# A decoder trunk's FFN: four segments of 11 blocks with three fours per layer by seven products, turns in pairs, and zero matmuls in the last norm

## The chip, the cores and the metric

The kernel runs on one core of one Trainium2 chip. The time of a run is the device time in microseconds (us). PE is the tensor engine's matmuls, PEld its weight loads, DVE the vector engine, ACT the scalar engine, POOL GpSimd, and SP the engine whose queue issues the loads.

## The reference, cut to what matters

Two layers work on 256 positions of 2048 features: one with latent attention, one with dilated window attention. Each is followed by a feed-forward network with a short convolution, and after both layers comes a norm.

```python
def conv_ffn(h, w_up, conv_w, conv_b, w_down):
    u = h @ w_up                                  # 256 x 2048 by 2048 x 11264
    up = jnp.pad(u, ((0, 0), (2, 0), (0, 0)))
    c = conv_b + up[:, 0:S] * conv_w[0]
    for j in range(1, 3):
        c = c + up[:, j:j + S] * conv_w[j]
    gate, val = c[..., :5632], c[..., 5632:]
    return (jax.nn.silu(gate) * val) @ w_down     # 256 x 5632 by 5632 x 2048
...
for i in range(2):
    x = x + mixer(rms_norm(x, attn_norm[i]))
    x = x + conv_ffn(rms_norm(x, ffn_norm[i]), ...)
return rms_norm(x, final_norm)
```

The precision of float32 is kept by splitting each operand into a rounded part and a rest (high and low part) and adding three products.

## The kernel before, in words

The hidden width of 5632 is 44 blocks of 128 features. A block has a gate half and a value half. `up(fb)` makes both, one *unit* each: `load` brings 2048 columns of weights into a tile `w` (three buffers), ACT rounds them into tiles `wh` of 1024 columns (L91), DVE subtracts to get the rests `wl` (L92), with five buffers of each, and `proj` runs 16 matmuls of 512 columns over the high parts and 16 of 256 columns over the low parts, all at L135. `keep` then takes the sum out of PSUM (L211, L213), scales it, and `conv` applies the convolution: one ACT instruction (L949) and two on DVE (L953) per half, then silu on the gate half (L955), the product with the value half (L958), and `split_act` for high and low part (L346, L347). The result `gl[fb]` is one input of the down projection.

The down projection runs in segments of blocks (`SEGS`). `down(seg)` makes 16 chunks of 128 output features, one unit each, over the blocks of the segment. Each chunk's PSUM is seeded with half of the residual (L124), and `keep_residual` (L365, L367) writes the sum back into it. A segment is done after two blocks of the next one. In the last segment the first two chunks run over all inputs but the last before anything else, so that the last block has time to be finished.

Some groups of four blocks are not made by `up` but by `seven(fb0)`: the product of 2x2 blocks by Strassen's scheme in Winograd's form, 7 products instead of 8. Its stationary operands are sums of input chunks, made once per layer by `make_forms` (DVE L816 to L819, L347), for eight pairs of chunks, one in every fourth unit from the third one on. Six of the products run inside the segment that is computed at that time: after each of the 16 down units one function of `mains` is called, in turn `first(kk)` (12 matmuls, L845 to L847) and `second(kk)` (6 matmuls). `first` loads 1 MB for the pair in two halves (L865), subtracts on DVE (L873), and makes high and low parts (ACT L872, L874, DVE L875, L876); `second` makes one more difference and its parts (L884 to L887). `sums` adds the products up, `third` runs the seventh product in two halves, and `turn(f)` turns a block from positions by features to features by positions: four transposes into the one PSUM bank `pt` (L938) and the convolutions of both halves out of it.

The order of the work around this is given by the list `steps`: `unit` runs a projection, then calls the next step, then evacuates the projection before. Instructions are put into each engine's queue by a planner that follows the order of the program as far as operands and buffers are free in its own reckoning; each engine then works its queue in that order.

At the end `rstd_x` sums the squares by four matmuls, takes the root on POOL, `spread` copies the two columns over all partitions by four matmuls (L290), and DVE scales the 16 chunks, which are then stored (L1037, L1038). The kernel begins with nine matmuls on zeros (L232).

Of the kernel before, what the change touches and what calls it, by code (L numbers as in the profile page):

```python
# [18 lines left out]
F32 = mybir.dt.float32  # L19
F32R = mybir.dt.float32r  # L20
BF16 = mybir.dt.bfloat16
# [5 lines left out]
P = 128  # L27
T = 256
# [9 lines left out]
GROUPS = ((128, 1), (512, 4), (2048, 16))  # L38
FFN = 5632
FB = FFN // P  # L40
SEGS = ((0, 14), (14, 28), (28, 44))
HALF = 4 * P
SEVEN = (16, 30)
NEG = -1.0e30


# [6 lines left out]
def trunk_kernel(tc, x_d, pos_d, gain_d, conv_d, const_d, mask_d, wqa_d, wkva_d, wqb_d, wkvb_d, wo_d,  # L53
                 win_d, dwo_d, wup_d, wdn_d, out_d):
    nc = tc.nc
    with ExitStack() as ctx:
# [6 lines left out]
        work = ctx.enter_context(tc.tile_pool(name="work", bufs=4))  # L63
        small = ctx.enter_context(tc.tile_pool(name="small", bufs=4))
        pp = ctx.enter_context(tc.tile_pool(name="pp", bufs=4, space=PSUM))
        pss = ctx.enter_context(tc.tile_pool(name="pss", bufs=2, space=PSUM))
# [121 lines left out]
        steps = []  # L188
# [4 lines left out]
        def together(*fs):  # L193
            return lambda: [f() for f in fs]

        def flush():
            while pending:
                e, ps = pending.pop(0)
                e(ps)
# [27 lines left out]
        zero = work.tile([P, T], F32, name="zero", tag="lo", bufs=2)  # L227
        nc.vector.memset(zero, 0.0)
        zero = zero.bitcast(BF16)
        idle = pss.tile([P, 512], F32, name="idle", tag="ps")  # L230
        for _ in range(9):
            nc.tensor.matmul(idle, zero[:, :P], zero, start=True, stop=True)  # L232

        load_x(0, 1, nc.scalar)
        nc.scalar.dma_start(gains, gain_d)
# [40 lines left out]
        def sumsq(name, paired=False, last=None):  # L276
            acc = state[name]
            acc = acc.rearrange("p (a e) -> p e a", e=2) if paired else acc.rearrange("p (e a) -> p e a", e=2)
            ps = pso.tile([P, 512], F32, name="po", tag="po")
            for tt in range(2):  # L280
                nc.tensor.matmul(ps[:, tt:tt + 1], acc[:, tt, :], ones, start=True, stop=last is None)
                if last is not None:
                    nc.tensor.matmul(ps[:, tt:tt + 1], last[:, ts(tt, P)], ones, start=False, stop=True)
            return ps[:, 0:2]

        def spread(col, name, pool):

            ps = pso.tile([P, 512], F32, name="po", tag="po")
            for tt in range(2):
                nc.tensor.matmul(ps[:, ts(tt, P)], col[:, tt:tt + 1].to_broadcast([P, P]), ident,  # L290
                                 start=True, stop=True)
            if pool is None:
                return ps[:, :T]
            t = pool.tile([P, T], F32, name=name, tag=name)
            nc.vector.tensor_copy(t, ps[:, :T])
            return t

        def rstd_x(paired=False, last=None):
            ps = sumsq("x", paired, last)
            ms = small.tile([P, 2], F32, name="ms", tag="ms")  # L300
            nc.vector.tensor_scalar(ms, ps, 1.0 / D, EPS, op0=ALU.mult, op1=ALU.add)
            r = small.tile([P, 2], F32, name="rcol", tag="rcol")
            nc.gpsimd.tensor_tensor(r, ms, negh, op=ALU.pow)
            return r
# [57 lines left out]
        def keep_residual(k, ps, paired=False):  # L362

            t = work.tile([P, T], F32, name="lo", tag="lo", bufs=2)
            nc.scalar.activation(t, ps[:, T:], AF.Copy)  # L365
            hi, lo = (a.rearrange("p (e a) -> p e a", e=2) for a in (ps[:, :T], t))
            nc.vector.tensor_add(tokens(k, paired), hi, lo)  # L367
# [418 lines left out]
        def ffn(layer, goff, ready):  # L786
            gl = {}
            rb = {}
# [177 lines left out]
            def up(fb):  # L966
                for i in range(2):
                    w = load(wup_d[layer, fb * 2 + i], D, tok=D)
                    unit(lambda: proj(w, xs, KC), lambda ps, i=i: keep(fb, i, ps))

            def down(seg):
                a, b = SEGS[seg]

                def finish(c, ps):
                    keep_residual(c, ps)
                    if seg == len(SEGS) - 1:
                        ready(c)

                gs, n = [gl[f] for f in range(a, b)], b - a
                c = 0  # L980
                if seg == len(SEGS) - 1:

                    early = []
                    for c in range(2):
                        w = load(wdn_d[layer, c, :, a * P:b * P], n * P, tok=D)
                        early.append((w, proj(w, gs, n, upto=n - 1, onto=tokens(c))))
                    for c, (w, ps) in enumerate(early):
                        finish(c, proj(w, gs, n, since=n - 1, ps=ps))
                    c = 2
                for c in range(c, KC):  # L990
                    w = load(wdn_d[layer, c, :, a * P:b * P], n * P, tok=D)
                    unit(lambda: proj(w, gs, n, onto=tokens(c)), lambda ps, c=c: finish(c, ps))
                    if mains:
                        mains.pop(0)()
                        state["run"] = 0
# [3 lines left out]
            for fb in range(FB):  # L999
                if any(f <= fb < f + 4 for f in SEVEN):  # L1000
                    continue
                up(fb)
                if seg < len(SEGS) - 1 and fb == SEGS[seg][1] + 1:
                    mains, sums, thirds, last_sum, turns = seven(fb + 1)
                    down(seg)
                    seg += 1
                    sums()
                    steps.extend([nothing, *thirds, last_sum, nothing, *turns])
            flush()
            down(seg)  # L1010
            flush()
# [4 lines left out]
        with tc.tile_pool(name="ffn0", bufs=1) as fpool:  # L1016
            ffn(0, G_FFN, lambda c: chunk_ready(c, G_ATTN + KC, paired=True))
# [3 lines left out]
        last = small.tile([P, T], F32, name="last", tag="sq", bufs=1)  # L1021
# [7 lines left out]

        with tc.tile_pool(name="ffn1", bufs=1) as fpool:  # L1030
            ffn(1, G_FFN + KC, final)
        rb = spread(rstd_x(last=last), "rb", None)
        cuts = [0, 1] + list(range(2, KC + 1, 2))
        for a, b in zip(cuts, cuts[1:]):
            x = xq[a // 4][:, a % 4 * T:(a % 4 + b - a) * T]
# [84 lines left out]
```

## Time and profile before

| | |
|---|---|
| median of 3 runs | 2684.89 us (2684.44 to 2685.51) |
| the profiled execution | 2684.24 us |
| its span, first to last instruction | 2682.5 us |
| PE, DVE, ACT busy | 99%, 76%, 59% of the span |
| granted clock of PE, mean | 0.998 |
| loads from memory | 497.30 MB, 186 GB/s over the span |

A granted clock of 1.00 is 2.4 GHz, 0.50 is 1.2 GHz. Matmuls are pipelined and their ends are modelled, so that neighbours overlap; the spacing of their starts is what one costs.

### The profile page before, as it was taken

What the parts mean: (1) busy time and instruction counts of PE and PEld (TensorE: products, weight loads), DVE (VectorE), ACT (ScalarE), POOL (GpSimd) and SP (SyncE); (2) the same over time, 40 slices, a digit from 0 to 9 for tenths busy, and PEclk for the clock granted to TensorE, in tenths of its full rate; (3) what the DMA queues carried; (4) which work ended last, traced back from release to release, by engine and by line L of the source; (5) the groups of instructions that cost most, each with busy time, mean ns of one, the idle gap of its engine ahead of it and who ended that gap; (6) DMA issues with size and microseconds to landing.
All of it is one profiled execution on the core that took longest, in us unless ns stands there. A gap on an engine that the chain in (4) does not pass through costs nothing.

```text
span 2682.5 us, 39684 instructions
## 1 busy us (share of the span) xinstructions
PE 2666.1 (99%) x15301; PEld 2352.1 (88%) x15301; DVE 2035.6 (76%) x3479; ACT 1587.2 (59%) x2478; POOL 24.2 (1%) x39
## 2 busy tenths in 40 slices
PE   9999999999999999999999999999999999999998
PEld 7998888888888888898888888888888888888887
DVE  7987888789788766676577667667688878978874
ACT  6775666566666654444454444445666666666664
POOL 2000000000000000000000000000000000000000
PEclk9999999999999999999999999999999999999999
DMA  6345555665665555544544544554555566566553
GB/s 246 138 137 202 186 191 188 202 220 188 197 226 190 199 188 199 178 172 170 192 169 166 196 158 172 189 173 161 190 187 189 190 203 219 186 200 226 189 190 124
DMA packets 125901, 501.97 MB, mean 187 GB/s; under 512 B 10000, under 2 KB 60560, under 8 KB 85136
## 3 DMA queue, kind: packets, MB, share of 16 engines
q1 hardware_dynamic: 125424, 499.26, 54.3%
q8 instruction: 120, 1.97, 0.3%
q14 instruction: 69, 0.57, 0.1%
q10 hardware_dynamic: 288, 0.18, 0.0%
HBM read 497.30 MB, written 2.10 MB: 186 GB/s over the span
## 4 chain that ended last, share of the span: by engine, by line
PE 70%; issue 27%; DVE 0%; ACT 0%; POOL 0%; POOLq 0%; DVEq 0%; ACTq 0%
PE pp L135 51%; PE pp L163 3%; PE pp L165 3%; PE pp L164 3%; PE pp L104 1%; PE pp L106 1%; PE pp L105 1%; PE po L773 1%; PE ps L736 1%; PE ps L845 0%; PE ps L846 0%; PE ps L847 0%; PE ps L104 0%; PE ps L106 0%; PE ps L105 0%
## 5 line engine op out<-in xcount | busy, mean ns | idle before, releaser
L92 DVE TENSOR_TENSOR wl<-w,wh 128x1024 fp32r<-128x1024 f32 (+2 forms) x770 | 913.2, 1195 | 398.4 <-ACT wh L91 269.7
L91 ACT ACTIVATE wh<-w 128x1024 fp32r<-128x1024 f32 (+2 forms) x770 | 792.7, 1033 | 383.9 <-PE pp L135 246.3
L135 PE MATMUL pp<-xs,wh 128*128 128x512 f32 x3904 | 917.5, 391 | 0.0
L135 PEld LDWEIGHTS pp<-xs,wh 128*128 128x128 f32 x3904 | 724.0, 188 | 144.4
L135 PEld LDWEIGHTS pp<-xs,wl 128*128 128x128 f32 x3904 | 486.7, 192 | 9.8
L135 PE MATMUL pp<-xs,wl 128*128 128x256 f32 x3904 | 494.9, 284 | 0.0
L135 PE MATMUL pp<-a,wh 128*128 128x512 f32 x1920 | 454.4, 390 | 0.0
L135 PEld LDWEIGHTS pp<-a,wh 128*128 128x128 f32 x1920 | 357.8, 188 | 72.3
L135 PEld LDWEIGHTS pp<-a,wl 128*128 128x128 f32 x1920 | 244.0, 191 | 7.7
L135 PE MATMUL pp<-a,wl 128*128 128x256 f32 x1920 | 247.9, 283 | 0.0
L211 ACT ACTIVATE lo<-pp 128x256 f32<-128x256 f32 x241 | 92.2, 382 | 130.0 <-PE pp L135 129.2
L153 DVE TENSOR_TENSOR wl<-w,wh 128x1024 fp32r<-128x1024 f32 x96 | 116.2, 1218 | 62.8 <-ACT wh L152 50.6
L953 DVE SCALAR_TENSOR_TENSOR cv<-upad,convs,cv 128x256 f32<-128x256 f32 x288 | 138.4, 482 | 28.1 <-ACT cv L949 24.3
L152 ACT ACTIVATE wh<-w 128x1024 fp32r<-128x1024 f32 x96 | 101.6, 1058 | 97.2 <-PE pp L164 48.7
L163 PE MATMUL pp<-wh,xs 128*128 128x512 f32 x384 | 150.1, 391 | 0.0
L165 PE MATMUL pp<-wl,xs 128*128 128x512 f32 x384 | 149.6, 389 | 0.0
L164 PE MATMUL pp<-wh,xs 128*128 128x512 f32 x384 | 149.5, 389 | 0.0
L949 ACT ACTIVATE cv<-upad,convs 128x256 f32<-128x256 f32 x144 | 86.1, 599 | 94.0 <-DVE upad L963 92.3
L124 ACT ACTIVATE pp<-x 128x512 f32<-128x512 f32 x112 | 67.3, 601 | 84.0 <-DVE x L367 80.2
L213 DVE TENSOR_TENSOR sum<-pp,lo 128x256 f32<-128x256 f32 x241 | 101.1, 419 | 0.7 <-ACT lo L211 0.6
L873 DVE TENSOR_TENSOR t<-w 128x1024 f32<-128x1024 f32 x32 | 39.2, 1225 | 73.0 <-DMA w<-in_wup 73.0
L165 PEld LDWEIGHTS pp<-wl,xs 128*128 128x128 f32 x384 | 72.1, 188 | 15.1
(294 smaller groups left out, 2732.2 us busy)
## 6 DMA issues: line engine op xcount, KB each, us to landing
w<-in_wup SPq DMA_DIRECT2D x144, 1024.0 KB, 4.7
w<-in_win SPq DMA_DIRECT2D x96, 1024.0 KB, 4.7
w<-in_wdn SPq DMA_DIRECT2D x64, 896.0 KB, 4.6
w<-in_win SPq DMA_DIRECT2D x96, 512.0 KB, 4.1
w<-in_wup SPq DMA_DIRECT2D x64, 512.0 KB, 5.2
w<-in_wdn SPq DMA_DIRECT2D x32, 1024.0 KB, 4.9
w<-in_wo SPq DMA_DIRECT2D x16, 1024.0 KB, 4.7
w<-in_dwo SPq DMA_DIRECT2D x16, 1024.0 KB, 4.7
```

Source lines behind the costliest of these rows:

```text
L91: nc.scalar.activation(h, w[:, c:e], AF.Copy)
L92: nc.vector.tensor_sub(l, w[:, c:e], h.bitcast(F32))
L135: nc.tensor.matmul(ps[:, i * T:], w_k, xs[k][:, :(2 - i) * T], start=(k == 0 and i == own), stop=(k == n - 1), skip_group_check=(i != own))
L152: nc.scalar.activation(wh4, src, AF.Copy)
L153: nc.vector.tensor_sub(wl4, src, wh4.bitcast(F32))
L163: nc.tensor.matmul(ps, xh, wh, start=k == 0, stop=False)
L164: nc.tensor.matmul(ps, xl, wh, start=False, stop=False)
L165: nc.tensor.matmul(ps, xh, wl, start=False, stop=k == KC - 1)
L211: nc.scalar.activation(t, ps[:, T:], AF.Copy)
L213: nc.vector.tensor_add(u, ps[:, :T], t)
L949: nc.scalar.activation(c, u[:, 2:] if padded else u, AF.Identity, scale=convs[:, cw + 2:cw + 3], bias=convs[:, cw + 3:cw + 4])
L953: nc.vector.scalar_tensor_tensor(o, v, convs[:, cw + j:cw + j + 1], o, op0=ALU.mult, op1=ALU.add)
```

## The change

`SEGS` and `SEVEN` are set anew: four segments of 11 blocks, and three fours (blocks 13 to 16, 24 to 27 and 35 to 38) by seven products, where there were two fours in segments of 14, 14 and 16. The four turns of a four are called in two steps of two, in the seventh and the ninth unit after the sums, instead of in the sixth to ninth. The zero matmuls get a function of their own, and five each are put ahead of the sums of squares of the last norm and behind them. The formula for which blocks are made where is not changed otherwise.

```diff
-SEGS = ((0, 14), (14, 28), (28, 44))
+SEGS = ((0, 11), (11, 22), (22, 33), (33, 44))
 HALF = 4 * P
-SEVEN = (16, 30)
+SEVEN = (13, 24, 35)
...
         idle = pss.tile([P, 512], F32, name="idle", tag="ps")
-        for _ in range(9):
-            nc.tensor.matmul(idle, zero[:, :P], zero, start=True, stop=True)
+
+        def busy(n):
+            for _ in range(n):
+                nc.tensor.matmul(idle, zero[:, :P], zero, start=True, stop=True)
+
+        busy(9)
...
                     sums()
-                    steps.extend([nothing, *thirds, last_sum, nothing, *turns])
+                    steps.extend([nothing, *thirds, last_sum, nothing, nothing, together(*turns[:2]), nothing, together(*turns[2:])])
...
             ffn(1, G_FFN + KC, final)
-        rb = spread(rstd_x(last=last), "rb", None)
+
+        zero = work.tile([P, T], F32, name="zero", tag="lo", bufs=2)
+        nc.vector.memset(zero, 0.0)
+        zero = zero.bitcast(BF16)
+        idle = pss.tile([P, 512], F32, name="idle", tag="ps")
+        busy(5)
+        r = rstd_x(last=last)
+        busy(5)
+        rb = spread(r, "rb", None)
```

`together(*fs)` calls its functions one after the other as a single step.

## Rows read from the trace of the kernel before

**Rows 1.** The page: busy time, share of the span, instructions.

```profile
PE 2666.1 (99%) x15301; PEld 2352.1 (88%) x15301; DVE 2035.6 (76%) x3479; ACT 1587.2 (59%) x2478; POOL 24.2 (1%) x39
```

**Rows 2.** Waits of PE (seven rows): us in total, times, longest.

```profile
PE pp L516 <- DVE xs L260: 1.4, 1, 1.4
PE po L283 <- ACT last L1027: 1.3, 1, 1.3
```

**Rows 3.** Chain of waits, first layer's FFN: start us, us, what.

```profile
451.53 4.85 PE pp L135 x28
...
465.36 4.85 PE pp L135 x28
...
568.40 5.54 PE pp L135 x32
...
599.48 0.63 PE pt L938 x4
...
605.90 0.44 PE pt L938 x4
```

**Rows 4.** Windows, first down segment: PE, PEld, DVE, ACT, POOL busy, clock, DMA.

```profile
443.80:554.40 110.60, 110.60 (x593) 95.89 (x592) 85.79 (x100) 68.97 (x93) 0.00 (x0) 1.00 0.64 203
```

**Rows 5.** Timeline, first and fourth turn: start us, us, engine, line, instruction.

```profile
593.21 0.60 PE L938 MATMUL pt<-cst,t 128*128 128x128 f32 x4
...
595.97 0.99 DVE L953 SCALAR_TENSOR_TENSOR cv<-pt,convs,cv 128x254 f32<-128x254 f32 x2
...
597.38 0.55 ACT L949 ACTIVATE cv<-pt,convs 128x256 f32<-128x256 f32 x1
...
613.93 0.60 PE L938 MATMUL pt<-cst,t 128*128 128x128 f32 x4
...
621.90 0.76 DVE L347 TENSOR_TENSOR a<-cv,a 128x256 fp32r<-128x256 f32 x2
```

**Rows 6.** Timeline of the first down segment; in brackets the idle time before.

```profile
441.59 0.93 SPq L865 DMA_DIRECT2D w<-in_wup  x2
...
447.47 1.23 DVE L873 TENSOR_TENSOR t<-w 128x1024 f32<-128x1024 f32 x1 [0.46 <-DMA w<-in_wup]
...
462.79 1.23 DVE L873 TENSOR_TENSOR t<-w 128x1024 f32<-128x1024 f32 x1 [2.59 <-DMA w<-in_wup]
...
499.65 0.93 SPq L865 DMA_DIRECT2D w<-in_wup  x2
...
506.08 1.23 DVE L873 TENSOR_TENSOR t<-w 128x1024 f32<-128x1024 f32 x1 [3.25 <-DMA w<-in_wup]
...
514.14 0.93 SPq L865 DMA_DIRECT2D w<-in_wup  x2
...
535.86 1.23 DVE L873 TENSOR_TENSOR t<-w 128x1024 f32<-128x1024 f32 x1 [4.23 <-DMA w<-in_wup]
...
537.01 0.95 DVE L92 TENSOR_TENSOR wl<-w,wh 128x768 fp32r<-128x768 f32 x1
...
537.50 1.83 PE L135 MATMUL pp<-a,wl 128*128 128x256 f32 x14
```

**Rows 7.** Groups by line and shape on DVE: busy us, mean ns, idle before.

```profile
L347 DVE TENSOR_TENSOR forms<-t,forms 128x512 fp32r<-128x512 f32 x16 | 11.0, 686 | 1.4 <-ACT forms L346 1.4
...
L819 DVE TENSOR_TENSOR t<-y,t 128x128 f32<-128x128 f32 x16 | 4.7, 292 | 0.6
```

**Rows 8.** Timeline of PE: a spreading in mid run, and the end.

```profile
1003.02 0.60 PE L290 MATMUL po<-cst,rcol 128*128 128x128 f32 x4
...
2665.07 3.82 PE L135 MATMUL pp<-a,wh 128*128 128x512 f32 x16
...
2672.11 1.23 PE L290 MATMUL po<-cst,rcol 128*128 128x128 f32 x4 [1.02 <-POOL rcol L303]
```

**Rows 9.** Window at the end, columns as in rows 4.

```profile
2672.10:2673.40 1.30, 1.23 (x4) 0.93 (x4) 0.02 (x1) 0.00 (x0) 0.00 (x0) 0.50 0.00 0
```

**Rows 10.** Groups by line on PE: the zero matmuls at the start.

```profile
L232 PE MATMUL idle<-zero 128*128 128x512 bf16 x9 | 4.0, 631 | 1.2 <-DVE zero L228 1.2
```

## The prediction

> **What bounds the kernel now.** I read the page first: the tensor engine (PE) counts as busy for 99% of the span [rows 1]. Busy is not yet bound, so the next view is what PE waits for: the longest wait in the whole run is 1.4 us, and there are seven waits in all [rows 2]. PE therefore sets the time in every stage. A change pays only by taking matmuls off PE, and only as long as the other engines still deliver weights and inputs in time. The chain of waits gives the prices. A unit of the up projection (32 matmuls) takes 5.54 us, a unit of a down segment with 14 blocks (28 matmuls) 4.85 us, and two such units with the seven products between them repeat every 465.36 - 451.53 = 13.83 us [rows 3]. The windows show that the vector engine (DVE) comes next, with 85.8 of 110.6 us in a down segment [rows 4]. The rest of the profile is read for two delays that PE does not feel yet: how long a turned block is on its way [rows 5], and how late a load of the products is [rows 6].
>
> **The change part by part.**
>
> *One more four per layer by seven products.* It takes away eight up units, 8 x 5.54 = 44.3 us of PE. It adds 7 x 8 x 3 = 168 matmuls of 512 columns: of the period of 13.83 us, two down units take 9.70 us, so the 18 matmuls between them take 4.13 us, 0.229 us each, and 168 take 38.5 us. It adds four turns of four transposes. The chain holds 0.63 us for one and 0.44 us for another [rows 3]; at 0.44 for three of the four, 2.0 us. Net: 44.3 - 38.5 - 2.0 = 3.8 us per layer, 7.6 us in both. That is what PE can win at most here.
>
> *Four segments instead of three.* The blocks add up to 44 either way, so PE's matmuls in the down units stay the same. Each layer gets 16 more seeds and 16 more residual sums on ACT and DVE, which run beside PE: nothing, as long as DVE keeps up. Per period DVE now works 85.8 / 8 = 10.7 us. In each of two down units the second piece shrinks from 768 to 384 columns. 768 and 1024 columns cost 0.95 and 1.23 us [rows 6], so 384 cost some 0.55, and DVE needs 9.9 us. PE's period becomes 13.83 - 6 x 4.85 / 14 = 11.75 us. On average there is room (84%).
>
> *The load loop of the products.* The average hides a chain that is slower than PE already. The load at L865 is issued at 499.65 and the next at 514.14: 14.49 us, against 13.83 for PE. That is 6.43 us from the issue to L873, which uses the load, and 8.06 us of DVE work from there until the slot is free and the next issue follows [rows 6]. Each pair thus loses some 0.6 us of the lead with which the segment began. At the eighth pair the piece of 768 behind L873 ends at 537.96. PE starts its run over the low parts at 537.50 and reaches that piece after 8 of 14 matmuls of 0.116 us, at 538.4. Half a microsecond is left.
>
> There are two readings from here. If DVE's order stays, the loop takes 14.4 (from 462.79 to 506.08 there are three) - 0.8 = 13.6 us and loses 1.85 us per pair, 2.8 in the first, which is 15.3 long before: 12 us by the eighth pair. The lead at the second pair was 451.53 + 14 x 0.231 + 8 x 0.116 less 447.47 + 1.23 + 0.95, 6.0 us; with units shorter by 1.04, a run of high parts shorter by 0.69 and a piece cheaper by 0.4, 4.7 us are left. PE would wait 7.3 us in each of six segments, 44 us. But the order is made anew for each kernel. L873 stands ahead of the second down piece because that piece's slot frees only when PE has used the first low piece of the unit before, 10.4 us into the period (4.85 + 1.38 + 3.23 + 0.93); with 11 blocks it frees 8.7 us into it, 4.0 us after the earliest issue of the load. At the segment's start the order holds eight DVE instructions, some 5 us, between the issue at 441.59 and L873 at 447.47: it was made for a load longer than 4 us. So the piece, and the low part at L887 with it, should come ahead of L873, the DVE part shrinks to about 5.7 us, and 5.7 + 6.2 = 11.9 us is level with 11.75. I take 0, the nearer by that row, and keep 44 as the far end.
>
> *The turned blocks of the third four.* The fours at 13 and 24 have 14 up units ahead of their down segment. The one at 35 has blocks 39 to 43, ten units, and the last pair of turns sits in the ninth. A turn needs the one bank `pt`: its transposes wait until the convolutions of the turn before have read it. From the first turn at 593.21 to the fourth at 613.93 that took 20.7 us, and the fourth block's input to the down projection was done at 622.66, 8.7 us later [rows 5]. In the changed kernel the first turn comes at the end of the seventh unit, three units and the transposes (17.9 us) before the end T of the last up unit. By the same spacing the fourth turn is at T + 2.8 and block 38 is ready at T + 11.5. With DVE free of other work the chain behind a turn adds up to 4.9 us (transposes, two convolutions on ACT, four on DVE, and three instructions of 0.42), and at the spacing of the first two (6.27 us) the fourth turn comes at T + 0.9: T + 6. The last down segment needs block 38 as its sixth input, 1.2 us after T. PE can put the first four inputs of the second and third chunk ahead (8 x 0.231 = 1.8 us), so it waits from T + 3 until between T + 6 and T + 11.5: 3 to 8.5 us per layer. I take the middle, 5.75, since loads thin out once PE stands, but block 43's own evacuation shares DVE: 11.5 us in both layers.
>
> That two turns stand in one step does not shorten this. The second half's convolution starts on ACT at 597.38 only after DVE's two reads of the same bank, which began at 595.97 and took 0.99 [rows 5]. The Trainium skill says why ("PSUM — Partial Sum Buffer", "PSUM bank collisions raise a hardware error"): two engines may not even read one bank together, so accesses are guarded by bank. The trace agrees; by that rule a pair on one bank does not overlap, where two turns side by side would have brought block 38 6.3 us earlier.
>
> *The clock behind that stall.* At the end of the run PE's dense matmuls are over at 2668.9. After 2672.10 the granted clock is 0.50 (1.2 GHz), and there four spreading matmuls take 1.23 us where the same four took 0.60 at 1003.02, at 2.4 GHz [rows 8, 9]. At the start nine zero matmuls took 4.0 us, 0.45 us each, the lower level again [rows 10]. A wait of some 6 us in mid kernel could be followed by as long a stretch at the lower level, worth half of its 4 us. Bounds 0 and 2 us per layer; I take 1.5, 3 us in all. The Trainium skill speaks here against the change ("TensorE: Matmul & The Clock Gate", "HAM oscillation — how this bites in real kernels"): a PE that has waited long starts its next work throttled. The end of this trace agrees; by the rule the sum is 3 us higher than without it.
>
> *Forms.* With 26 instead of 32 units ahead of the first four, the forms of the last two pairs fall into the first down segment: DVE 4 x 0.29 + 0.69 = 1.9 us each [rows 7]. DVE's 16% of room, 1.9 us per period, covers it; without that cover it costs up to 2 us per layer. I take 0.
>
> *Zero matmuls in the last norm.* Five run while the last square is made: PE's wait there is 1.3 us [rows 2], five at 0.23 are 1.15, hidden. Five run while POOL makes the root, in a gap of 1.02 us: 0.1 over. If they hold the clock, the spreading falls from 1.23 to 0.60: -0.5 us in all. If not, the five take 2.2 us: +1.2.
>
> **The sum.** -7.6 (PE) + 0 (loop) + 11.5 (last fours) + 3.0 (clock) + 0 (forms) - 0.5 (norm) = +6.4 us on the profiled execution's 2684.24 (span 2682.5 and 1.7 around it; the median of the runs is 0.65 above): 2690.6 us, +0.24%. About 0.2%, 5.4 us, is what a measurement of this kernel can tell from no change.
>
> **Rivals.**
> - *The gain comes through* (0.22). Block 38 is ready by T + 3: the order would have to give the turns DVE without pieces of 1.23 us between, and let PE run other chunks longer. Then -7.6 - 0.5 = -8.1: 2676 us, up to 2679 with a stall of 1.3 us per layer, where it decides: below that the kernel is faster by over 0.2%. For it: a wait on PE is paid only where it ends last, and the early chunks were made to cover a late block. Against it: they cover less now, 11 inputs instead of 16.
> - *The load loop binds as well* (0.22). From 1 us in each of six segments to 7.3: the forecast + 6 to + 44, 2697 to 2735 us. For it: half a microsecond was left before. It decides where L873 is over 11.75 us behind the one before, pair after pair.
> - *The forecast* (0.50): 2682 to 2698 (stalls of 3 to 8.5, clock 0 to 2 per layer, the norm's bounds).
> - *The change does not save its matmul time* (0.06): turns and sums fill what the sevens free, 2684 to 2687.
>
> **How the numbers follow.** The forecast has a little over half of its weight above 2690, the rest within 0.2%. Slower: 0.22 of the loop and 0.27 of the forecast, 0.49. Same: 0.23 and the 0.06, 0.29. Faster: 0.22. The range runs from 2676 to 2708 and leaves out the upper part of the loop's case.
>
> **What would show it.** Right: PE's matmuls add up to some 8 us less; PE waits several us at L135 in the last down segment of each layer, released by L346 or L347, with a granted clock under 1.00 behind it; the spreading takes 0.6 us. Wrong: no PE wait near the last down segments (then 2676); PE waits at L135 for low parts all through the down segments (then over 2697); two down units that do not repeat every 11.75 us.

## The result and the profile after

The changed kernel takes 2695.10 us (median of five, 2692.94 to 2697.76) where the kernel before takes 2684.97 (five, 2684.44 to 2685.51): ratio 1.0038, 95% interval 1.0027 to 1.0049. It is slower by 10.1 us. The profiled execution took 2694.99 us, with a span of 2693.2. One execution of run 6 below took 3776.88 us at a mean granted clock of 0.65 and is not counted in its range. In what is quoted from here on, lines below the new function `busy` stand four lines lower than before: the load at L865 is L869, the subtraction at L873 is L877, the split of an input to the down projection is L350 and L351.

The page after, its line for busy time, beside [rows 1]:

```profile
PE 2666.9 (99%) x15167; PEld 2342.6 (87%) x15167; DVE 2109.9 (78%) x3630; ACT 1644.1 (61%) x2624; POOL 23.7 (1%) x39
```

PE has 134 matmul instructions fewer although ten are new in the norm, so it has 144 fewer in the layers, 72 in each. Its busy time did not fall: matmuls at the lower clock (4.5 us, below) and the ten zero matmuls (0.215 us each) use up most of what the 144 free. Waits come on top, which are not busy time. These are the waits of PE (us in total, times, longest), beside [rows 2]:

```profile
PE pp L135 <- ACT a L350: 7.4, 2, 3.7
PE pp L135 <- ACT pp L124: 4.9, 4, 3.6
```

Neither stood among the seven of before. The first is the wait forecast ahead of the last down segment, once in each layer. The second was not forecast. It stands at the starts of the second and third segment, and what it waits for is a seed: ACT's instruction at L124, which puts the residual into the bank in which a down unit then adds. The clock falls as well. In the windows after (length, PE, PEld, DVE, ACT and POOL busy, granted clock, DMA share, GB/s) the first line is the first down segment, for [rows 4], the other two are what follows the wait ahead of the last segment in each layer:

```profile
410.88:503.59 92.71, 92.71 (x491) 79.80 (x489) 81.71 (x106) 63.80 (x94) 0.00 (x0) 1.00 0.62 215
...
938.70:942.20 3.50, 3.50 (x14) 3.06 (x14) 2.69 (x7) 1.75 (x5) 0.00 (x0) 0.51 0.00 0
2618.10:2625.00 6.90, 6.28 (x22) 5.70 (x23) 4.38 (x11) 3.07 (x7) 0.00 (x0) 0.51 0.03 5
```

In the first segment PE is busy for 92.71 of 92.71 us at the full clock. The load loop does not hold it, nor do the forms. Behind the two waits the clock is 0.51 for 3.5 and 6.9 us. Matmuls of 512 columns start 0.43 us apart there instead of 0.23, and the two stretches lose 1.5 and 3.0 us by such spacings.

The chain of waits in that segment, for [rows 3]: the first of the two down units of every period.

```profile
417.59 3.81 PE pp L135 x22
...
429.58 3.81 PE pp L135 x22
...
441.33 3.81 PE pp L135 x22
```

441.33 - 429.58 = 11.75 us, the period that was worked out from before's 13.83.

The timeline ahead of the last down segment of the first layer, for [rows 5] (start us, us, instruction; in brackets the idle time before and what ended it):

```profile
930.33 0.39 PE L135 MATMUL pp<-a,wh 128*128 128x512 f32 x1
930.56 0.60 PE L942 MATMUL pt<-cst,t 128*128 128x128 f32 x4
...
932.07 0.56 ACT L953 ACTIVATE cv<-pt,convs 128x256 f32<-128x256 f32 x1
...
933.38 0.99 DVE L957 SCALAR_TENSOR_TENSOR cv<-pt,convs,cv 128x254 f32<-128x254 f32 x2
...
934.79 0.55 ACT L953 ACTIVATE cv<-pt,convs 128x256 f32<-128x256 f32 x1
...
937.50 0.42 ACT L350 ACTIVATE a<-cv 128x256 fp32r<-128x256 f32 x1 [1.68 <-DVE cv L962]
...
937.97 0.50 PE L135 MATMUL pp<-a,wl 128*128 128x256 f32 x2 [3.72 <-ACT a L350]
```

The segment begins at 930.33, and the fourth turn's transposes stand inside it, 0.23 us later: the turn before reads the one bank until 930.23. Its block passes ACT and DVE in turn, the second half behind the first, and its input is split 6.9 us after the transposes. PE has meanwhile used what it had and starts no matmul from 933.85 to 937.97. The second layer shows the same, 2614.61 to 2618.72.

The start of the second segment, after. This is the wait that nobody looked for:

```profile
585.00 1.22 DVE L877 TENSOR_TENSOR t<-w 128x1024 f32<-128x1024 f32 x1
...
593.34 0.68 DVE L889 TENSOR_TENSOR t<-t,w 128x512 f32<-128x512 f32 x1
...
594.10 1.86 SPq L869 DMA_DIRECT2D w<-in_wup  x2
...
603.05 1.22 DVE L877 TENSOR_TENSOR t<-w 128x1024 f32<-128x1024 f32 x1 [3.87 <-DMA w<-in_wup]
...
604.39 1.06 ACT L878 ACTIVATE wh<-t 128x1024 fp32r<-128x1024 f32 x1 [4.47 <-DVE t L877]
605.36 0.58 ACT L124 ACTIVATE pp<-x 128x512 f32<-128x512 f32 x1
...
605.99 2.33 PE L135 MATMUL pp<-a,wh 128*128 128x512 f32 x9 [3.61 <-ACT pp L124]
```

Read it from the bottom. PE needs the seed of L124. The seed itself, by the trace, waits only for its place on ACT: it stands behind L878, which waits for L877, which waits for the load issued at 594.10. That load could only go out when L889 had read the slot of the pair before, at 594.02. A wait of the *products* so stops a *down unit* which has no data in common with them. The same chain of waits gives the transfer 8.08 us:

```profile
594.53 8.08 DMA w<-in_wup
```

That is the second half of the load; the median of the second halves is 5.2 us. PE's starts are 3.99 us apart there, 0.76 at the third segment, and 0.71 and 1.00 in the second layer. At those three starts the load goes out as late, but lands in the usual time. The third segment's, which begins at 773.25:

```profile
777.05 0.93 SPq L869 DMA_DIRECT2D w<-in_wup  x2
...
782.82 1.23 DVE L877 TENSOR_TENSOR t<-w 128x1024 f32<-128x1024 f32 x1 [0.64 <-DMA w<-in_wup]
```

So a late load alone costs PE 0.5 to 0.8 us, and the 3.8 us come where the load is late and also long. The profiles of runs 3, 4 and 9 below show the same: in each, one start has a second half of 8.2 to 8.7 us and PE's starts 4.1 to 4.3 us apart, and the others have 5.2 to 5.4 us and 0.7 to 1.3. In all four long cases the issue of the two halves took 1.8 to 2.0 us (1.86 above) instead of 0.93, and a 16 KB transfer of the queue for instructions (q8) lay over it. Whether that transfer makes the load long was not tested.

The end, for [rows 8]:

```profile
2680.12 1.24 PE L234 MATMUL idle<-zero 128*128 128x512 bf16 x5
...
2683.37 0.71 PE L294 MATMUL po<-cst,rcol 128*128 128x128 f32 x4
```

The four spreading matmuls take 0.71 us where they took 1.23.

### The profile page after: what moved, and what is told of

It reads as the page before. It is cut to its first block, busy times and chain, and to the rows that moved or that the text cites. A ratio compares the mean times of both kernels' runs of the same rounds, so it can differ in the third digit from the quotient of the medians.

```text
span 2693.2 us, 40103 instructions
## 1 busy us (share of the span) xinstructions
PE 2666.9 (99%) x15167; PEld 2342.6 (87%) x15167; DVE 2109.9 (78%) x3630; ACT 1644.1 (61%) x2624; POOL 23.7 (1%) x39
## 4 chain that ended last, share of the span: by engine, by line
PE 93%; DVE 2%; DMA 1%; ACT 1%; issue 0%; SPq 0%; DVEq 0%; ACTq 0%
PE pp L135 68%; PE pp L163 3%; PE pp L164 3%; PE pp L165 3%; PE ps L850 1%; PE ps L851 1%; PE ps L849 1%; DMA w<-in_wup 1%; PE pp L104 1%; PE pp L106 1%; PE pp L105 1%; PE pp L849 1%; PE pp L850 1%; PE pp L851 1%; PE po L777 1%; PE ps L740 1%
## 5 line engine op out<-in xcount | busy, mean ns | idle before, releaser
L92 DVE TENSOR_TENSOR wl<-w,wh 128x1024 fp32r<-128x1024 f32 (+2 forms) x802 | 881.5, 1110 | 364.7 <-ACT wh L91 230.5
L91 ACT ACTIVATE wh<-w 128x1024 fp32r<-128x1024 f32 (+2 forms) x802 | 771.4, 966 | 359.9 <-PE pp L135 217.5
L135 PE MATMUL pp<-xs,wh 128*128 128x512 f32 x3648 | 858.1, 390 | 0.0
L135 PEld LDWEIGHTS pp<-xs,wh 128*128 128x128 f32 x3648 | 676.3, 188 | 135.3 <-DVE xs L264 0.2
L135 PE MATMUL pp<-a,wh 128*128 128x512 f32 x1920 | 464.6, 392 | 4.9 <-ACT pp L124 4.9
L135 PE MATMUL pp<-xs,wl 128*128 128x256 f32 x3648 | 465.3, 284 | 0.0
L135 PEld LDWEIGHTS pp<-xs,wl 128*128 128x128 f32 x3648 | 455.8, 191 | 9.4
L957 DVE SCALAR_TENSOR_TENSOR cv<-upad,convs,cv 128x256 f32<-128x256 f32 x256 | 122.0, 480 | 18.8 <-ACT cv L953 16.2
L124 ACT ACTIVATE pp<-x 128x512 f32<-128x512 f32 x144 | 85.4, 594 | 22.4 <-DVE x L371 21.4
L877 DVE TENSOR_TENSOR t<-w 128x1024 f32<-128x1024 f32 x48 | 58.8, 1224 | 45.5 <-DMA w<-in_wup 44.7
```

Of the source, the lines that this page charges most:

```text
L91: nc.scalar.activation(h, w[:, c:e], AF.Copy)
L92: nc.vector.tensor_sub(l, w[:, c:e], h.bitcast(F32))
L124: nc.scalar.activation(dst, onto.unsqueeze(1).to_broadcast([P, 2, 2, P]), AF.Copy, scale=0.5)
L135: nc.tensor.matmul(ps[:, i * T:], w_k, xs[k][:, :(2 - i) * T], start=(k == 0 and i == own), stop=(k == n - 1), skip_group_check=(i != own))
L957: nc.vector.scalar_tensor_tensor(o, v, convs[:, cw + j:cw + j + 1], o, op0=ALU.mult, op1=ALU.add)
```

## The experiments

All are compared with the kernel before, run on the same chips (2684.5 to 2684.7 us). Diffs are against the changed kernel where nothing else is said.

**1. Turned blocks earlier.**

```
-steps.extend([nothing, *thirds, last_sum, nothing, nothing, together(*turns[:2]), nothing, together(*turns[2:])])
+steps.extend([nothing, *thirds, last_sum, together(*turns[:2]), nothing, together(*turns[2:])])
```

> The changed kernel with the two pairs of turns two units earlier (after the fifth and the seventh unit instead of the seventh and the ninth). Theory A (the turned blocks of the third four come too late for the last down segment, and the stall lowers the clock behind it): the fourth turn moves from 930.6 to some 919.5, block 38 is ready before the last up unit ends; the gaps of 4.1 us at 933.9 and 2614.6 and the stretches of 3.4 and 6.8 us at the lower clock go: 7.8 + 5.1 = 12.9 us less, 2682 us. Theory B (DVE has too much to do in the ten units ahead of the last segment, whenever the turns stand): the wait stays at some 4 us per layer, wherever it falls, 2693 to 2697. Theory C (the waits for the second load at the start of the second and third segment are the larger part): 2690 or more, since they stay.

Measured: 2675.19 us (2674.82 to 2675.98), ratio 0.9964, interval 0.9951 to 0.9977: faster than the kernel before, and 7 us better than my theory's number. Neither of the two new waits is left, and the FFN runs at the full clock throughout. The theory had only the wait ahead of the last segment in it. The starts of the second and third segment went with it, and this timeline of the second segment's start says how:

```profile
580.14 1.23 DVE L877 TENSOR_TENSOR t<-w 128x1024 f32<-128x1024 f32 x1
...
587.51 0.93 SPq L869 DMA_DIRECT2D w<-in_wup  x2
...
593.28 1.22 DVE L877 TENSOR_TENSOR t<-w 128x1024 f32<-128x1024 f32 x1
...
599.75 1.04 ACT L878 ACTIVATE wh<-t 128x1024 fp32r<-128x1024 f32 x1
601.01 0.60 ACT L124 ACTIVATE pp<-x 128x512 f32<-128x512 f32 x1
```

The segment begins at 590.17, as it did in the changed kernel (590.25). But the first pair's subtraction comes 4.9 us earlier and the second pair's load 6.6 us earlier, since the convolutions of the last two turned blocks (fourth turn at 556.60, in the changed kernel at 567.78) are out of DVE's way. The load then lands ahead of its use.

**2. Two banks for the turned blocks.**

```
-pt = pst.tile([P, 512], F32, name="pt", tag="pt")
+pool, name = ((pst, "pt"), (pso, "po"))[f % 2]
+pt = pool.tile([P, 512], F32, name=name, tag=name)
```

> The changed kernel with every second turn in the bank po instead of pt, so that the two turns of a pair need not wait for each other. Theory A, with the single bank as the reason for the spacing: the second and fourth turn follow the first and third at once, block 38 is ready 4 to 6 us earlier, the gap of 4.1 us falls under 1 us and the clock stays: 2682 to 2687. If the spacing comes from DVE and ACT and not from the bank: the turns are earlier, but the input of block 38 (L351) is not, 2693 to 2697.

Measured: 2676.60 us (2676.20 to 2677.34), ratio 0.9969, interval 0.9957 to 0.9980. Again better than expected, for the same reason. The places of the steps are the change's, but the two turns of a pair now start 0.44 us apart (920.12 and 920.56), where on one bank they were 6.2 us apart (924.33 and 930.56). The prediction's reading of the pairs holds: on one bank they do not overlap. The Trainium skill ("PSUM — Partial Sum Buffer", "PSUM bank collisions raise a hardware error") has accesses guarded by bank, and the trace agrees.

**3. Without the third four.** Four segments, but blocks 35 to 38 by plain products.

```
-SEVEN = (13, 24, 35)
+SEVEN = (13, 24)
...
-mains, sums, thirds, last_sum, turns = seven(fb + 1)
+if fb + 1 in SEVEN:
+    mains, sums, thirds, last_sum, turns = seven(fb + 1)
```

> Four segments of 11 with the fours at 13 and 24 alone; blocks 35 to 38 are made by up units, and the third segment has no products in it. PE has the same matmuls as the kernel before. Theory A: no stall ahead of the last segment, no lower clock; the extra segment costs nothing but the wait for the second load in the second segment (3.8 and 0.5 us in the profile of the change): 2684.5 (before, less 0.5 in the norm) + 1 to 4, 2685 to 2689. If segments of 11 cost by themselves (seeds, residual sums, shorter units): 2692 or more.

Measured: 2693.29 us (2690.54 to 2696.10), ratio 1.0032, interval 1.0020 to 1.0045. A miss for both theories. The wait ahead of the last segment is gone, but waits for the seed at the second segment's start are there (PE's starts 1.0 us apart in the first layer, 4.3 in the second, with the clock at half behind it). The late pairs of the four at 13 stand ahead of that start. Behind those of the four at 24 comes a segment that has no products here, and PE does not wait at its start. This run first showed that the starts are a term of their own.

**4. Zero matmuls in the gap** ahead of the last segment: sixteen of 512 columns, into a bank that nothing reads.

```
+fill(16)
 for c, (w, ps) in enumerate(early):
     finish(c, proj(w, gs, n, since=n - 1, ps=ps))
```

> The changed kernel with 16 zero matmuls in the gap ahead of the last segment, which keep PE busy and compute nothing. Clock as I have it: the granted clock stays 1.00 behind the gap, 1.7 and 3.4 us less, 2690 us, and the gap itself stays. If the clock's record is without effect on the matmuls: 2695 as before.

Measured: 2694.29 us (2692.53 to 2696.13), ratio 1.0035, interval 1.0022 to 1.0048. 0.8 us below the change, within the spread of both, where 2690 was expected: the time says little, and a gain is not shown. It would fit the other reading too, a clock without effect on the matmuls, but that one fails on their spacing in the changed kernel's low stretches (0.43 us against 0.23). The windows say more: the last segments of both layers, and what follows the start of the second segment.

```profile
929.00:942.00 13.00, 12.59 (x62) 8.77 (x61) 11.08 (x24) 8.16 (x18) 0.00 (x0) 1.00 0.26 92
2606.00:2626.00 20.00, 19.59 (x109) 15.22 (x109) 15.74 (x36) 12.82 (x29) 0.00 (x0) 1.00 0.35 109
...
605.50:612.00 6.50, 6.48 (x21) 5.42 (x22) 3.24 (x5) 3.39 (x5) 0.00 (x0) 0.54 0.27 74
```

With PE kept at work the clock stayed at 1.00 behind the late block in both layers of this execution, so it is the waiting that takes it down. It fell behind the start of the second segment (a gap of 4.09 us) instead, which it had not done behind 3.99 us in the changed kernel's profile.

**5. The kernel before with early turns in pairs** (diff against the kernel before).

```
-steps.extend([nothing, *thirds, last_sum, nothing, *turns])
+steps.extend([nothing, *thirds, last_sum, together(*turns[:2]), nothing, together(*turns[2:])])
```

> The kernel before (three segments, fours at blocks 16 and 30) with the turned blocks in pairs and directly behind the last sum, as in the run with the earlier turns. Theory (the earlier turns only take away two waits that the fourth segment brought, and the gain against the kernel before is the third four's): before has neither wait, so nothing changes, 2684 to 2686. Rival (early turns in pairs are worth something by themselves, whatever the segments): 2677 to 2681, most of the gain of that run without a third four.

Measured: 2683.43 us (2682.67 to 2686.11), ratio 0.9996, interval 0.9987 to 1.0005: no change. Early turns are worth nothing where no late turn costs.

**6. Early turns, no third four**: the edits of 1 and 3 together.

> Four segments and earlier turns in pairs, but the third four left to plain products (fours at blocks 13 and 24 alone). Theory: with the waits away the third four is worth what its matmuls are, 3.8 us a layer, so this run is 7.6 above the 2675.2 with the third four: 2682.8, between 2681 and 2684.5, and its TensorE count is some 140 higher. Rival (segments or early turns bring the gain, the third four little): 2675 to 2678.

Measured: 2683.91 us (2683.44 to 2686.61), ratio 0.9997, interval 0.9988 to 1.0007. With run 1 this prices the third four undisturbed: 2683.91 - 2675.19 = 8.7 us. The fourth segment, which this run has and the kernel before has not, costs nothing.

**7. Early turns, no zero matmuls in the norm.**

```
-busy(5)
-r = rstd_x(last=last)
-busy(5)
-rb = spread(r, "rb", None)
+rb = spread(rstd_x(last=last), "rb", None)
```

> Earlier turns, without the ten zero matmuls and their memset in the last norm. Theory: the spreading of the last norm goes back from 0.71 to about 1.23 us at the half clock, and the time goes up by 0.5: 2675.7, between 2675.3 and 2676.2. Rival (the stretch is not on the path, or the zeros cost what they bring): 2675.2 or less.

Measured: 2675.82 us (2675.07 to 2676.22), 0.6 above run 1. The medians differ as expected, the ranges touch; the spreading, which took 0.71 us, shows the cause:

```profile
2664.11 1.22 PE L294 MATMUL po<-cst,rcol 128*128 128x128 f32 x4 [1.02 <-POOL rcol L307]
```

**8. Early turns and two banks**: 1 and 2 together.

> Earlier turns and two banks for the turned blocks together. Theory: each alone takes the same waits away, so together they are worth no more than the better of them: 2674.5 to 2676, and no gap over 0.5 us between the starts of TensorE's instructions in the FFN but those of the norms. Rival (the bank is a cost of its own, some 0.7 us a four at the first pair): 2671 to 2673.5.

Measured: 2674.75 us (2674.44 to 2675.84), ratio 0.9963, interval 0.9951 to 0.9976. No more than run 1 alone, as expected. With run 1 it is the fastest version here.

**9 and 10. Early turns for one kind of four alone.** In run 9 for the last four, in run 10 for the first two (`<` in place of `==`):

```
+wait = [] if fb + 1 == SEVEN[-1] else [nothing, nothing]
+steps.extend([nothing, *thirds, last_sum, *wait, together(*turns[:2]), nothing, together(*turns[2:])])
```

> The turned blocks of the last four alone stand directly behind the last sum; those of the first two fours stay where the change has them. Theory (the change's loss is two separate terms, the last four's turned blocks with the clock that falls behind their wait, and the starts of the second and third segment): the last four's 7.8 and 5.1 us go, the starts' 5.5 stay, so 2675.2 + 5.5 = 2680.7, between 2679 and 2684.5 (a wait of 4 us at a start may take the clock down for 1.7 to 3.4 us). Rival (one term alone, whatever its place: the late turns of any four make all of it): either 2675 to 2677 or above 2690.

> The reverse: the turned blocks of the first two fours early, those of the last four as the change has them. Theory: the starts' waits go, the last four's stay: 2675.2 + 7.8 + 5.1 = 2688.1, between 2686 and 2690, with gaps of 3.5 to 4.2 us ahead of the last segment's products in each layer and the clock at half behind them. Rival (one term alone): 2675 to 2677, or above 2693.

Measured: run 9 2683.77 us (2679.91 to 2685.30), ratio 0.9996, run 10 2688.14 us (2687.03 to 2689.21), ratio 1.0012, interval 1.0003 to 1.0022. Both as expected. Their longest waits of PE, run 9 first, then run 10:

```profile
PE pp L135 <- ACT pp L124: 5.4, 4, 3.9
```

```profile
PE pp L135 <- ACT a L350: 7.4, 2, 3.7
```

Each has one of the two waits whole and nothing of the other. Above run 1 they lie by 8.6 and 12.95 us, 21.5 together, where the changed kernel, which has both, lies by 19.9. Two terms, nearly additive, and the one that I had not foreseen makes some two fifths of what is lost. Run 9 spreads over 5.4 us and run 10 over 2.2, which fits that the starts depend on how long a transfer takes and the late block on ACT and DVE alone.

**11. Turns one at a time**, as the kernel before lists them.

```
+steps.extend([nothing, *thirds, last_sum, nothing, *turns])
```

> The change with its turned blocks one at a time, as the kernel before lists them (a free place behind the last sum, then four turns). The last turn's place is the same fifth one, but nothing shares it, so it should start some 6 us earlier than the change's fourth turn. Theory: the wait at the last segment is the pairs' second turn and goes nearly away, the first turns are earlier too: 2676 to 2683. Rival (the pairs don't matter, the shorter segments do): 2692 to 2697.

Measured: 2677.83 us (2677.01 to 2679.57), ratio 0.9975, interval 0.9964 to 0.9985. The fourth turn starts at 923.10, 7.5 us earlier than in pairs though it has the same place, the fifth step behind the last sum; block 38 is split by 931, and PE waits nowhere in the FFN for over 0.5 us. "Two blocks at a time", with the places that this list gives the pairs, is then the part that made the change lose: without it, the change would have won 6.7 us.

**12. Short segments**, with early turns, to find where the load loop binds.

```
-SEGS = ((0, 11), (11, 22), (22, 33), (33, 44))
+SEGS = ((0, 9), (9, 18), (18, 28), (28, 44))
-SEVEN = (13, 24, 35)
+SEVEN = (11, 20, 30)
```

> Earlier turns, and segments of 9, 9, 10 and 16 blocks instead of four of 11, so that the period of a pair of down products falls from 11.75 us to some 10.4 (9 blocks) and 11.1 (10). Theory of the prediction (the load loop, a load's issue to the release of its buffer, is 11.9 us long and just covered by 11.75): the period stays at 11.75 or more, 8 pairs lose 1.4, 1.4 and 0.7 us against TensorE's work, 28 us a layer, and the whole is some 50 to 60 us above the run with the earlier turns: 2725 to 2735. Rival (the loop is shorter than 10.4 us, its 11.9 was TensorE's own period read back): the periods are 10.4 and 11.1, and the time 2673 to 2679.

Measured: 2695.02 us (2691.58 to 2697.26), ratio 1.0035, interval 1.0021 to 1.0049. Between the two theories, so neither is right. The windows of the first two down segments, and the waits of PE:

```profile
388.69:472.23 83.54, 82.10 (x426) 69.74 (x425) 76.75 (x109) 59.93 (x94) 0.00 (x0) 1.00 0.63 206
537.34:622.21 84.87, 83.17 (x426) 69.62 (x425) 73.70 (x101) 55.80 (x88) 0.00 (x0) 1.00 0.61 203
```

```profile
PE pt L851 <- DVE wl L880: 4.3, 6, 0.8
PE ps L851 <- DVE wl L879: 2.7, 3, 2.1
```

By TensorE's work alone, 92.5 (a segment of run 1) less 16 chunks x 2 blocks x 3.81 / 11 us, a segment would take 81.4 us. These two take 83.5 and 84.9, and PE now does wait for low parts of the products. The load goes out at 555.14 and, five pairs later, at 607.28: 10.4 us per round. That is also TensorE's own period with 9 blocks, and single rounds take 9.4 to 11.4 us. So the loop is shorter than 11.9 us, but this run does not show where it binds: DVE is busy for 76.75 of 83.54 us in the first segment and waits for the load only once there, 0.6 us. Whether PE waits for late loads or for the mere amount of DVE's work is not separated. The six segments of a run lose some 8 us in the first layer and 11 in the second against that reckoning, nearly all of the 19.8 by which this run lies above run 1.

## Why the prediction was right, and where it was not

The sign and the main mechanism held: the change is slower by over 0.2%, and the largest loss is PE waiting for block 38 ahead of the last down segment of each layer, with half a clock behind it. 2695.1 lies 4.5 us above the predicted 2690.6 and within its range. That it comes so near is in part luck: the stall was put 3.7 us too high, and a term of 5.5 us that is not in the sum made up for it. Term by term:

- **PE, -7.6.** Runs 6 and 1 give -8.7, 4.3 us per layer instead of 3.8: slightly undersized. The count (72 matmul instructions per layer) is exact. The 0.5 us per layer lie in the turns. The prediction took 0.63 and 0.44 us, the lengths of two pieces of the chain, but what one costs is the time from the start of its transposes to the next matmul's. The first turn's transposes start at 593.21 [rows 5], the next matmul at 593.56, 0.35 us later. The mean of before's 16 turns is 0.36, so four take 1.45 us and not 2.0, and the sum becomes 44.3 - 38.5 - 1.45 = 4.35. The sign that PE's matmuls add up to 8 us less does not show in the busy time, which the lower clock and the zero matmuls fill up again.
- **The load loop, 0.** Right for the steady state, at 11.75 us per period. The order was made anew, as argued (L877 now comes behind the second down piece and the low part, L891), and the far end of 44 did not happen. The length of 11.9 us was too long: from load to load single rounds take 9.6 us in the changed kernel (463.82 to 473.45) and 9.4 in run 12, so there was more room than "level". Where the loop binds stays open.
- **The turned blocks of the third four, +11.5.** The mechanism was right in its steps: the fourth turn came at T + 0.2 (forecast T + 0.9 to 2.8), block 38 at T + 7.2 to 7.6 (T + 6 to 11.5), the wait began at T + 3.5 (T + 3). Only the size was off: gaps of 4.11 us between starts that are else 0.23 apart, 2 x 3.9 = 7.8 us.
- **The clock behind it, +3.0.** 1.5 + 3.0 = 4.5 us in the profiled execution, 1.4 + 1.4 in run 10's. (The expectations of the runs have 5.1, which takes half of each stretch as lost.) The bound of 2 us per layer was too low, since a low stretch can be 6.8 us long. The Trainium skill's rule ("TensorE: Matmul & The Clock Gate", "HAM oscillation — how this bites in real kernels") spoke rightly against the change: the trace agrees, with a granted clock of 0.51 behind both waits, and 1.00 there in run 4, where zero matmuls filled the wait.
- **Forms, 0**, and the fourth segment's seeds and sums, nothing: right (the first segment's window; run 6).
- **Norm, -0.5.** Right: 0.6 between the medians of runs 7 and 1, whose ranges overlap, and 0.5 in the spreading itself (1.22 and 0.71).
- **What failed** is a step that is in the prediction only as a half sentence: "the fours at 13 and 24 have 14 up units ahead of their down segment". It was read as room enough, because their turned blocks are ready in time for the down units. So they are. But the work of a late pair stands on DVE just where the first products of the next segment are to be prepared, and what is late next is the second pair's load, then a subtraction, then the seed behind it on ACT's queue. 3.76 + 0.53 + 0.48 + 0.77 = 5.5 us in the profile (the four distances between starts less 0.23), 8.6 in run 9 against run 1. Some 3 us of the first is the load's own long time, for which run 1's load, out 6.6 us earlier, leaves room. The load loop was costed for its rhythm, not for its start.

The sum with measured terms: -8.7 - 0.6 + 7.8 + 4.5 + 5.5 = +8.5 us, against +10.1 between the medians and +10.75 between the profiled executions. Where the remaining 1.6 to 2.2 us lie was not followed up. Why one load at a segment's start takes 8 us, where 5.2 is the median of second halves, is not explained.

## What to carry to other kernels

A change that saves work on the engine that sets the time is worth what the latest of its side products leaves of it: the 8.7 us were there, and a place of two steps in a list decided whether they came as a gain of 9.5 or a loss of 10. When a stall is looked for, follow a late piece of work also to those who don't need its data: whoever stands behind it in the order of DVE or ACT, and what load waits for them. And two pieces of work that share one PSUM bank are in series, however they are listed; put together in one late step they end later than one by one in four.

## What the runs showed of the hardware

- The granted clock did not answer alike to like gaps. Behind gaps of 4.09 to 4.27 us between PE's starts it fell to 0.5 each time, for 3.4 us or for 6.8; behind one of 3.99 it did not fall, and in run 12 it fell for 3.4 us behind one of 2.48. Behind the same gap of 4.11 us in the second layer, the low stretch was 6.8 us in the changed kernel's profile and 3.4 in run 10's. Part of the spread between runs of one kernel may be that; no run separates it.
- At the lower level matmuls of 512 columns (fp32r) started 0.427 us apart, at the full clock 0.23: a low stretch of 3.4 us loses some 1.5 us, a little under half.
- Matmuls of 512 columns (fp32r) in the products started 0.23 us apart at the full clock, the zero matmuls of 512 columns (bf16) in the norm 0.21 to 0.22 (five between 2680.12 and 2680.98).
- The first half of a load of products (512 KB) took 4.0 to 4.8 us from issue to landing in the changed kernel's profile, the second 5.1 to 8.1, with 5.2 as the median. A step that sits on it needs the long one covered.
- Over all profiles, the issue of such a half took over 0.9 us in 27 of 1216 cases, each time with a transfer of the instruction queue (q8) over it. Without one it took at most 0.7. The four loads of over 8 us are among the 27; most of the others landed within 6.4 us.
